# Six of eight blocks of an up-projection with the weights stationary and 256 tokens moving

## The chip, the core and the metric

The kernel runs on one NeuronCore of a Trainium2 chip. Five engines work side by side, each through its own instructions in order: TensorE (PE, which multiplies matrices; its weight loads are listed apart as PEld), VectorE (DVE), ScalarE (ACT), GpSimd (POOL) and SyncE (SP), which here issues nearly all the DMAs. The metric is the device time of one execution in microseconds, less is better.

## The reference

One transformer block on 256 tokens of width 2048: an adaptive normalisation, two attention mixers, an output projection, and a feed-forward part of width 8192. Only the feed-forward part is touched by the change:

```python
h = modulate(rms_norm(x, pre_norm_ffn[l]), shift_f, scale_f)     # 256 x 2048
f = jnp.square(jax.nn.relu(h @ w_up[l])) @ w_down[l]             # w_up 2048 x 8192, w_down 8192 x 2048
x = x + gate_f[:, None, :] * rms_norm(f, post_norm_ffn[l])
```

All of it is in fp32. The kernel splits an operand into a rounded part `hi` (the type fp32r) and a remainder `lo`, and takes three fp32r products, hi·hi, hi·lo and lo·hi, for one product (`products`, L548).

## The kernel before

A matrix multiplication here has a stationary operand of 128 x 128, loaded into PE ahead (LDWEIGHTS), and a moving one of 128 rows and up to 512 columns. The result has the stationary operand's columns as partitions and the moving one's columns along them.

**Up-projection.** The sums over 2048 inputs (16 steps k of 128) run in four groups of four k (`F_GROUPS`, L53; the loop at L1174). In each group eight blocks (`blk`, L1178) of 1024 output features follow one another. For one k of one block `weight_units` (L461) loads 128 x 1024 weights by DMA, splits them into `up_<k>hi` on ACT (L544) and `up_<k>lo` on DVE (L545), and multiplies (`half`, L486): for each of the two halves t of 128 tokens, and for each half ci of 512 features, the tokens (`xmhi`, `modf4hi`, ... and their lo) are stationary and 512 features move. That is 4 PSUM banks per block, one for each (ci, t), and 3 x 4 = 12 matmuls of 512 columns for one k. The banks come in turn from five (`MM_BANKS`, L62), the split weights from five buffers (`WBUFS`, L64), so the weights of a k are split when those of five k earlier are used up. After the fourth k of a block `up_done` (L1153) takes a bank into `facc`: in the first group ACT copies it (L1160), in the others DVE adds it (L1162).

**Transposes.** With the tokens stationary, the sums lie with tokens on the partitions; the down-projection needs features there. So in the last group ACT takes the relu (L1164), and `squares` (L1139) transposes each of the 16 `facc` tiles by eight PE transposes of 128 x 128 (L1146, tile `ft`), which ACT squares on their way back (L1151). Sixteen such groups of eight stand on PE's queue, two inside each block but the first (`later_unit`, L1184) and two at the start of the down-projection (L1294).

**Down-projection.** 64 k of 128 features (`down_units`, L1245, tile `dps`), 24 matmuls of 512 columns each; ahead of every second one `fsplit` (L1197) splits `facc` into `fhi` and `flo`.

**What runs beside.** Inside groups 0 to 2 the scale and shift of the next four k of inputs are summed up on DVE (L323), transposed on PE (L377, `modf4t` in the first group), reduced on DVE (L379, `modf4red`), and put onto the inputs by ACT (L414, L417). A list scheduler puts the program in an order ahead of time, engine by engine; the order on each engine is then fixed.

Of the kernel before, what the change touches and what calls it, by code (L numbers as in the profile page):

```python
# [15 lines left out]
AF = mybir.ActivationFunctionType  # L16
# [3 lines left out]
P = 128  # L20
T = 256
NT = T // P
# [27 lines left out]

M_DIRECT = (3, 7, 11)
F_MODS = (4, 4, 4, 4)
F_GROUPS = ((0, 4), (4, 8), (8, 12), (12, 16))  # L53

F_FIRST = 1
# [3 lines left out]
GATE_K = 54  # L59
# [97 lines left out]
def tile_adaln_block(ctx: ExitStack, tc: tile.TileContext, x, c, w_ada, b_ada, g_pm, g_qm, w_in,  # L157
                     ck_pos, ck_w1, ck_w2, cv_pos, cv_w1, cv_w2, w_o, g_pf, g_qf, w_up, w_down,
                     rope, out):
    nc = tc.nc  # L160
# [101 lines left out]
    stream = Stream()  # L262
# [195 lines left out]
        return [[u] for u in units]  # L458


    def weight_units(name, wap, ks, col0, parts, stat, ps_of, done, spare=(), plain=0):  # L461

        ncol = parts[-1][0] + parts[-1][1]
        units = []
        for i0 in range(0, len(ks), 2):  # L470
            st = {}

            def load(i0=i0, st=st):
                st["raw"] = rawtile(f"{name}_{ks[i0]}")
                k = ks[i0]
                nc.sync.dma_start(
                    st["raw"][:, 0:2 * ncol].rearrange("p (k c) -> p k c", k=2),
                    wap[k * P:(k + 2) * P, col0:col0 + ncol].rearrange("(k p) c -> p k c", p=P))

            for kk in range(2):  # L480
                def prep(st=st, kk=kk, i0=i0):
                    hi, lo = split(st["raw"][:, kk * ncol:(kk + 1) * ncol], f"{name}_{ks[i0] + kk}",
                                   i0 + kk in spare)
                    st[kk] = (hi, lo)

                def half(t, st=st, kk=kk, i=i0 + kk):  # L486
                    k, first, last = ks[i], i == 0, i == len(ks) - 1
                    if k < plain:
                        raw, s32 = st["raw"], stat(k, t)
                    else:  # L490
                        whi, wlo = st[kk]
                        shi, slo = stat(k, t)
                    for ci, (off, wd) in enumerate(parts):
                        b = ps_of(ci, t, first)
                        cs = slice(off, off + wd)
                        if k < plain:
                            nc.tensor.matmul(b[:, 0:wd], s32,
                                             raw[:, kk * ncol + off:kk * ncol + off + wd],
                                             start=first, stop=last)
                        else:  # L500
                            products(b[:, 0:wd], shi, slo, whi[:, cs], wlo[:, cs], first, last)
                        if last:
                            done(ci, t, b)
                    stream.step()

                def main(half=half):
                    for t in range(NT):
                        half(t)

                unsplit = ks[i0] < plain  # L510
                u = Unit(load if kk == 0 else None, None if unsplit else prep, main,
                         w=0 if unsplit or i0 + kk in spare else 1,
                         free=None if kk == 0 else "main" if unsplit else "prep")
                u.half = half
                units.append(u)
        return units
# [28 lines left out]
        nc.vector.tensor_sub(lo[:, 0:n], src, hi[:, 0:n].bitcast(F32))  # L545
        return hi, lo

    def products(o, shi, slo, whi, wlo, first, last):  # L548
        nc.tensor.matmul(o, shi, whi, start=first, stop=False)  # L549
        nc.tensor.matmul(o, shi, wlo, start=False, stop=False)  # L550
        nc.tensor.matmul(o, slo, whi, start=False, stop=last)  # L551

    def banks(name):
        ps = {}
# [418 lines left out]
    def call(f):  # L973
        return [Unit(None, None, f)]
# [85 lines left out]
    def fs(k, t):  # L1060
        hi, lo = fstat[k // 2]
        return hi[:, k % 2, t * P:(t + 1) * P], lo[:, k % 2, t * P:(t + 1) * P]

    x2h = {"mod": {}}

    def keep_mod(k0, n, last):
# [86 lines left out]
    def up_done(blk, g):  # L1153
        def done(ci, t, b):
            n = blk * 2 + ci
            if n not in facc:
                facc[n] = chunk(f"facc{n}")
            dst = facc[n][:, t, :]
            if g == 0:
                nc.scalar.copy(dst, b)  # L1160
            else:
                nc.vector.tensor_add(dst, b, dst)  # L1162
            if g == len(F_GROUPS) - 1:
                nc.scalar.activation(dst, dst, AF.Relu)  # L1164
                if t == NT - 1:
                    later.append(n)
        return done

# [5 lines left out]
    for g, span in enumerate(F_GROUPS):  # L1174
# [3 lines left out]
        for blk in range(NB):  # L1178
            name = f"up{g}_{blk}"
            spare = ((1,), (1, 3))[blk] if g == 0 and blk < 2 else ()  # L1180
            us = weight_units(name, w_up, ks, blk * 1024, C2, fs, banks(name), up_done(blk, g),
                              spare)
            if lastg and blk:
                us = us[:2] + call(later_unit) + us[2:4] + call(later_unit) + us[4:]  # L1184
            base += us
        extra = [u for i, m in enumerate(ffn_mods) for u in m
# [58 lines left out]
    def down_units(k):  # L1245
# [31 lines left out]
        def half(t, order=(0, 1, 2, 3)):  # L1277
            hi, lo = fst[k // 2]
            ts_ = slice(t * P, (t + 1) * P)
            for n in order:  # L1280
# [10 lines left out]

    dn = [down_units(k) for k in range(KF)]
    token_major(dn[-4:], finish, 4)
    stream.add(2 * call(later_unit)  # L1294
               + spread(dn[:GATE_K], gf, 4, GATE_K - 2) + dn[GATE_K:GATE_K + 4]
               + [Unit(free="main")] + dn[GATE_K + 4:])
    stream.run()

# [24 lines left out]
```

## Time and profile before

| | |
|---|---|
| three runs, us | 1187.60, 1188.22, 1189.65; median 1188.22 |
| the profiled execution | 1188.98 us, of which the span of the core 1187.2 |
| PE busy in the span | 1154.3 us, 5411 matmuls |
| DVE, ACT busy | 901.4 and 592.8 us |
| DMA | 312 MB, 263 GB/s |
| up-projection, first to last matmul on the trace | about 457 to 825 us |
| down-projection | about 826 to 1180 us |

Busy time on PE counts pipelined matmuls whose ends are modelled, so that what a matmul costs is read from the distance between the starts of two that follow one another.

### The profile page before, as it was taken

How to read it: one execution, taken by the hardware profiler on the slowest of the kernel's cores; microseconds unless marked ns; L12 is line 12 of the kernel's file. 1: busy time of each engine (PE TensorE's matmuls, PEld its weight loads, DVE VectorE, ACT ScalarE, POOL GpSimd, SP SyncE). 2: the span in 40 equal slices, each digit the busy share in tenths (PEclk: the TensorE clock that was granted, in tenths of full speed). 3: DMA queues.
4: the chain of work that ended last, by engine and by line, in shares of the span. 5: the costliest groups of instructions: out<-in, count | busy, mean ns of one | idle time of the engine just before them, and what ended most of it. 6: DMA issues, size and time to landing. Idle time of an engine off the chain costs nothing.

```text
span 1187.2 us, 14413 instructions
## 1 busy us (share of the span) xinstructions
PE 1154.3 (97%) x5411; PEld 935.7 (79%) x5411; DVE 901.4 (76%) x1111; ACT 592.8 (50%) x908; POOL 13.5 (1%) x23
## 2 busy tenths in 40 slices
PE   5999999999999998999999999999999999999997
PEld 4468888877777786888888888888888888888885
DVE  5679999889999988777888986666576666665573
ACT  4353444438746658565343344767444434444441
POOL 1000000000000001000000000000000000000000
PEclk9999999999999999999999999999999999999999
DMA  9999998775867985988878976545677777775541
GB/s 333 370 394 326 334 362 295 238 281 176 316 213 258 327 337 200 367 285 305 290 249 300 315 248 204 172 152 208 238 244 270 255 258 264 259 268 187 203 142 71
DMA packets 92601, 312.03 MB, mean 263 GB/s; under 512 B 6306, under 2 KB 14962, under 8 KB 79602
## 3 DMA queue, kind: packets, MB, share of 16 engines
q1 hardware_dynamic: 92324, 311.04, 74.7%
q8 instruction: 42, 0.69, 0.2%
q14 instruction: 27, 0.22, 0.1%
q10 hardware_dynamic: 208, 0.07, 0.0%
HBM read 308.99 MB, written 2.10 MB: 262 GB/s over the span
## 4 chain that ended last, share of the span: by engine, by line
PE 88%; DVE 7%; ACT 1%; issue 1%; DMA 1%; POOL 0%; SPq 0%; DVEq 0%; POOLq 0%; ACTq 0%
PE dps L550 10%; PE dps L551 10%; PE dps L549 10%; PE up L551 9%; PE up L550 9%; PE up L549 9%; PE wo L550 2%; PE wo L549 1%; PE wo L551 1%; PE ft L1146 1%; PE in_qm L551 1%; PE in_qm L549 1%; PE in_qm L550 1%; PE in_km L549 1%; PE in_km L550 1%
## 5 line engine op out<-in xcount | busy, mean ns | idle before, releaser
L323 DVE SCALAR_TENSOR_TENSOR modm<-modm,csil,modm 128x1024 f32<-128x1024 f32 (+1 forms) x72 | 78.3, 1087 | 9.4 <-DMA modm<-in_w_ada_dram 8.0
L323 DVE SCALAR_TENSOR_TENSOR modf<-modf,csil,modf 128x1024 f32<-128x1024 f32 x60 | 76.8, 1280 | 5.6 <-DMA modf<-in_w_ada_dram 5.2
L1162 DVE TENSOR_TENSOR facc<-up,facc 128x512 f32<-128x512 f32 x96 | 61.5, 685 | 19.2 <-PE up L551 19.2
L323 DVE SCALAR_TENSOR_TENSOR gatef<-gatef,csil,gatef 128x1024 f32<-128x1024 f32 x32 | 40.6, 1280 | 1.7 <-DMA gatef<-in_w_ada_dram 1.7
L323 DVE SCALAR_TENSOR_TENSOR gatem<-gatem,csil,gatem 128x1024 f32<-128x1024 f32 x32 | 40.3, 1275 | 0.0
L1202 DVE TENSOR_TENSOR flo<-facc,fhi 128x512 fp32r<-128x512 f32 x32 | 21.8, 686 | 2.0 <-ACT fhi L1201 2.0
L1201 ACT CAST fhi<-facc 128x512 fp32r<-128x512 f32 x32 | 19.7, 624 | 5.3 <-PE up L550 1.9
L1164 ACT ACTIVATE facc<-facc 128x512 f32<-128x512 f32 x32 | 18.4, 623 | 2.8 <-DVE facc L1162 2.8
L1160 ACT COPY facc<-up 128x512 f32<-128x512 f32 x32 | 18.0, 586 | 1.7 <-PE up L551 1.0
L545 DVE TENSOR_TENSOR up_13lo<-up,up_13hi 128x1024 fp32r<-128x1024 f32 x8 | 9.8, 1226 | 11.5 <-ACT up_13hi L544 11.5
L545 DVE TENSOR_TENSOR up_14lo<-up,up_14hi 128x1024 fp32r<-128x1024 f32 x8 | 9.8, 1226 | 11.1 <-ACT up_14hi L544 11.1
L1151 ACT ACTIVATE facc<-ft 128x512 f32<-128x512 f32 x32 | 17.1, 586 | 0.4 <-PE ft L1146 0.2
L1146 PE MATMUL ft<-ident,facc 128*128 128x128 f32 x128 | 16.8, 273 | 0.0
L1146 PEld LDWEIGHTS ft<-ident,facc 128*128 128x128 f32 x128 | 14.7, 140 | 2.6 <-ACT facc L1151 0.4
L544 ACT CAST up_7hi<-up 128x1024 fp32r<-128x1024 f32 x8 | 8.4, 1056 | 14.2 <-PE up L551 14.2
L544 ACT CAST up_11hi<-up 128x1024 fp32r<-128x1024 f32 x8 | 8.4, 1056 | 14.2 <-PE up L551 14.2
L544 ACT CAST up_10hi<-up 128x1024 fp32r<-128x1024 f32 x8 | 8.4, 1056 | 13.3 <-PE up L551 13.3
L544 ACT CAST up_6hi<-up 128x1024 fp32r<-128x1024 f32 x8 | 8.4, 1056 | 13.3 <-PE up L551 13.3
L544 ACT CAST up_14hi<-up 128x1024 fp32r<-128x1024 f32 x8 | 8.4, 1049 | 12.6 <-PE up L551 12.6
L544 ACT CAST up_9hi<-up 128x1024 fp32r<-128x1024 f32 x8 | 8.4, 1056 | 12.1 <-DVE up_8lo L545 6.7
L544 ACT CAST up_8hi<-up 128x1024 fp32r<-128x1024 f32 x8 | 8.4, 1054 | 11.7 <-PE up L551 11.7
L544 ACT CAST up_5hi<-up 128x1024 fp32r<-128x1024 f32 x8 | 8.4, 1056 | 11.2 <-PE up L551 7.8
(2266 smaller groups left out, 3966.4 us busy)
## 6 DMA issues: line engine op xcount, KB each, us to landing
up<-in_w_up_dram SPq DMA_DIRECT2D x64, 1024.0 KB, 5.2
dn<-in_w_down_dram SPq DMA_DIRECT2D x64, 1024.0 KB, 5.0
modf<-in_w_ada_dram SPq DMA_DIRECT2D x64, 512.0 KB, 6.2
modm<-in_w_ada_dram SPq DMA_DIRECT2D x48, 512.0 KB, 7.1
gatem<-in_w_ada_dram SPq DMA_DIRECT2D x16, 1024.0 KB, 5.5
wo<-in_w_o_dram SPq DMA_DIRECT2D x16, 1024.0 KB, 6.3
gatef<-in_w_ada_dram SPq DMA_DIRECT2D x16, 1024.0 KB, 4.9
modm<-in_w_ada_dram SPq DMA_DIRECT2D x32, 256.0 KB, 6.0
```

Of the source, the lines that this page charges most:

```text
L323: nc.vector.scalar_tensor_tensor(part, w[:, j:j + step], csil[:, k:k + 1], part, ALU.mult, ALU.add)
L544: nc.scalar.copy(hi[:, 0:n], src)
L545: nc.vector.tensor_sub(lo[:, 0:n], src, hi[:, 0:n].bitcast(F32))
L549: nc.tensor.matmul(o, shi, whi, start=first, stop=False)
L550: nc.tensor.matmul(o, shi, wlo, start=False, stop=False)
L551: nc.tensor.matmul(o, slo, whi, start=False, stop=last)
L1146: nc.tensor.transpose(b[:, (2 * i + t) * P:(2 * i + t + 1) * P], f[:, t, (2 * j + i) * P:(2 * j + i + 1) * P], ident)
L1160: nc.scalar.copy(dst, b)
L1162: nc.vector.tensor_add(dst, b, dst)
L1164: nc.scalar.activation(dst, dst, AF.Relu)
L1201: nc.scalar.copy(hi, f)
L1202: nc.vector.tensor_sub(lo, f, hi.bitcast(F32))
```

## The change

In blocks 2 to 7 of every group the operands change places: 128 features of the weights are stationary and all 256 tokens move. A matmul has 256 columns in place of 512, and there are 24 for one k in place of 12. A bank (ci, t) now holds 2 x 128 features on the partitions and 256 tokens along each, which is the layout that the down-projection wants; so ACT takes the relu and then the square in place (L1189 of the changed kernel), and `squares` is left for the four `facc` tiles of blocks 0 and 1 alone. The two calls at the start of the down-projection go. Loads, splits, banks, and copies or adds out of the banks stay as many and as large as they were.

```diff
+UP_TOKENS = 2
@@ weight_units
+                    if across:
+                        whi, wlo = st[kk]
+                        xhi, xlo = stat(k)
+                        for ci, (off, wd) in enumerate(parts):
+                            b = ps_of(ci, t, first)
+                            for j in range(2):
+                                o = off + (2 * t + j) * P
+                                cs = slice(o, o + P)
+                                products(b[:, j * T:(j + 1) * T], whi[:, cs], wlo[:, cs], xhi, xlo,
+                                         first and j == 0, last, skip_group_check=True)
+                            if last:
+                                done(ci, t, b)
+                        stream.step()
+                        return
@@
+    def fs_all(k):
+        hi, lo = fstat[k // 2]
+        return hi[:, k % 2, :], lo[:, k % 2, :]
@@ up_done
             if g == len(F_GROUPS) - 1:
                 nc.scalar.activation(dst, dst, AF.Relu)
-                if t == NT - 1:
+                if blk >= UP_TOKENS:
+                    nc.scalar.activation(dst, dst, AF.Square)
+                elif t == NT - 1:
                     later.append(n)
@@
-            us = weight_units(name, w_up, ks, blk * 1024, C2, fs, banks(name), up_done(blk, g),
-                              spare)
-            if lastg and blk:
+            across = blk >= UP_TOKENS
+            us = weight_units(name, w_up, ks, blk * 1024, C2, fs_all if across else fs, banks(name),
+                              up_done(blk, g), spare, across=across)
+            if lastg and 0 < blk <= UP_TOKENS:
                 us = us[:2] + call(later_unit) + us[2:4] + call(later_unit) + us[4:]
@@
-    stream.add(2 * call(later_unit)
-               + spread(dn[:GATE_K], gf, 4, GATE_K - 2) + dn[GATE_K:GATE_K + 4]
+    stream.add(spread(dn[:GATE_K], gf, 4, GATE_K - 2) + dn[GATE_K:GATE_K + 4]
```

PE at the end of the up-projection, before: the last bank of block 7 (`up_7_1_1`, k 15), then transposes, which go on between the first matmuls of the down-projection (`dps`).

```order
L549 MATMUL up_7_1_1_6880<-up_7_15hi,modf12hi_6046 128x512
L550 MATMUL up_7_1_1_6880<-up_7_15lo,modf12hi_6046 128x512
L551 MATMUL up_7_1_1_6880<-up_7_15hi,modf12lo_6047 128x512
L1146 MATMUL ft_6964<-ident,facc_4726 128x128 x4
L1146 MATMUL ft_6969<-ident,facc_4726 128x128 x4
L1146 MATMUL ft_6976<-ident,facc_4799 128x128
L549 MATMUL dps_7001<-dn00hi,fhi_6920 128x512
L550 MATMUL dps_7001<-dn00lo,fhi_6920 128x512
L551 MATMUL dps_7001<-dn00hi,flo_6921 128x512
```

The same place in the changed kernel (L568 to L570 are its lines of `products`):

```order
L568 MATMUL up_7_1_1_7917<-modf12hi_6838,up_7_15hi 128x256
L569 MATMUL up_7_1_1_7917<-modf12lo_6839,up_7_15hi 128x256
L570 MATMUL up_7_1_1_7917<-modf12hi_6838,up_7_15lo 128x256
L568 MATMUL up_7_1_1_7917<-modf12hi_6838,up_7_15hi 128x256
L569 MATMUL up_7_1_1_7917<-modf12lo_6839,up_7_15hi 128x256
L570 MATMUL up_7_1_1_7917<-modf12hi_6838,up_7_15lo 128x256
L568 MATMUL dps_8032<-dn00hi,fhi_7924 128x512
L569 MATMUL dps_8032<-dn00lo,fhi_7924 128x512
L570 MATMUL dps_8032<-dn00hi,flo_7925 128x512
```

Three matmuls of 512 columns became six of 256, and the first product of the down-projection follows the last of the up-projection directly.

The scheduler also moves other work a little. ACT in the first group, before, at the end of block 4: the four copies out of block 4's banks (`facc<-up_4_...`) stand ahead of the work on the next inputs (`xnf`, `modf4hi`).

```order
L544 CAST up_5_3hi<-up_5_2_4418 128x1024
L1160 COPY facc_4526<-up_4_0_0_4459 128x512
L1160 COPY facc_4531<-up_4_1_0_4463 128x512
L1160 COPY facc_4526<-up_4_0_1_4467 128x512
L1160 COPY facc_4531<-up_4_1_1_4471 128x512
L414 ACTIVATE xnf_3920<-xnf_3920,modf4red 128x256 x2
L414 ACTIVATE xnf_3921<-xnf_3921,modf4red 128x256
```

ACT at the same place in the changed kernel:

```order
L563 CAST up_5_3hi<-up_5_2_4490 128x1024
L416 ACTIVATE xnf_3920<-xnf_3920,modf4red 128x256 x2
L416 ACTIVATE xnf_3921<-xnf_3921,modf4red 128x256
L419 CAST modf4hi_4901<-xnf_3920 128x512
L416 ACTIVATE xnf_3921<-xnf_3921,modf4red 128x256
L1183 COPY facc_4661<-up_4_0_0_4555 128x512
L419 CAST modf4hi_4907<-xnf_3921 128x512
L1183 COPY facc_4669<-up_4_1_0_4562 128x512
```

The copies now stand behind that work. On PE the eight transposes `modf4t` moved from the fourth k of block 4 into its third.

## Rows read from the trace of the kernel before

**Rows 1.** The page: busy time by engine; the granted clock in 40 slices.

```profile
PE 1154.3 (97%) x5411; PEld 935.7 (79%) x5411; DVE 901.4 (76%) x1111; ACT 592.8 (50%) x908; POOL 13.5 (1%) x23
...
PEclk9999999999999999999999999999999999999999
```

**Rows 2.** The page: the chain that ended last, by engine.

```profile
PE 88%; DVE 7%; ACT 1%; issue 1%; DMA 1%; POOL 0%; SPq 0%; DVEq 0%; POOLq 0%; ACTq 0%
```

**Rows 3.** Stages: window, length; busy PE, PEld, DVE, ACT, POOL; clock; DMA; GB/s.

```profile
550.00:630.00 80.00, 80.00 (x358) 66.28 (x357) 68.72 (x77) 34.59 (x37) 0.00 (x0) 1.00 0.81 285
630.00:737.00 107.00, 107.00 (x477) 88.61 (x476) 88.14 (x97) 44.71 (x46) 1.82 (x1) 1.00 0.76 263
737.00:825.00 88.00, 88.00 (x442) 73.97 (x442) 57.44 (x67) 61.06 (x89) 0.00 (x0) 1.00 0.52 178
...
832.00:1180.00 348.00, 346.45 (x1528) 286.40 (x1526) 211.21 (x204) 149.20 (x168) 0.55 (x1) 1.00 0.64 224
```

**Rows 4.** Waits of PE, whole span: us, times, longest.

```profile
PE up L549 <- ACT xmhi L417: 1.1, 1, 1.1
PE up L550 <- DVE up_2lo L545: 1.0, 1, 1.0
```

**Rows 5.** Waits of all engines, 550 to 640 us.

```profile
ACT up_7hi L544 <- PE up L551: 12.5, 7, 2.6
```

**Rows 6.** Line 1146: durations in ns, first and last start.

```profile
L1146 PE MATMUL ft<-ident,facc x128: 270/272/329, 742.7 to 830.4; 128*128 128x128 f32 x128
```

**Rows 7.** Timeline of PE around one group of transposes: start, length, instruction.

```profile
742.48 0.39 PE L551 MATMUL up<-up_13hi,modf12lo 128*128 128x512 f32 x1
742.71 1.03 PE L1146 MATMUL ft<-ident,facc 128*128 128x128 f32 x8
743.50 0.48 PE L549 MATMUL up<-up_14hi,modf12hi 128*128 128x512 f32 x1
...
744.28 0.39 PE L549 MATMUL up<-up_14hi,modf12hi 128*128 128x512 f32 x1
```

**Rows 8.** Timeline of PE from the up- to the down-projection.

```profile
825.04 1.14 PE L1146 MATMUL ft<-ident,facc 128*128 128x128 f32 x9
...
834.05 0.39 PE L551 MATMUL dps<-dn10hi,flo 128*128 128x512 f32 x1
```

**Rows 9.** Timeline of PE, 512 columns: the first and the 51st in a row.

```profile
700.55 0.39 PE L549 MATMUL up<-up_10hi,modf8hi 128*128 128x512 f32 x1
...
711.88 0.39 PE L551 MATMUL up<-up_10hi,modf8lo 128*128 128x512 f32 x1
```

**Rows 10.** Timeline of PE, 268 columns: the first and the 25th in a row.

```profile
117.07 0.28 PE L549 MATMUL in_kw<-in_kw_2hi,modm2hi 128*128 128x268 f32 x1
...
119.97 0.28 PE L549 MATMUL in_kw<-in_kw_4hi,modm2hi 128*128 128x268 f32 x1
```

**Rows 11.** Timeline of PE's weight loads just after the transposes of rows 7.

```profile
743.48 0.19 PEld L549 LDWEIGHTS up<-up_14hi,modf12hi 128*128 128x128 f32 x1
743.59 0.19 PEld L550 LDWEIGHTS up<-up_14lo,modf12hi 128*128 128x128 f32 x1
```

**Rows 12.** Timeline of ACT at the end of block 4, first group.

```profile
514.17 1.05 ACT L544 CAST up_3hi<-up 128x1024 fp32r<-128x1024 f32 x1 [1.67 <-PE up L551]
515.13 0.57 ACT L1160 COPY facc<-up 128x512 f32<-128x512 f32 x1
516.67 1.96 ACT L1160 COPY facc<-up 128x512 f32<-128x512 f32 x3 [0.97 <-PE up L551]
518.53 1.59 ACT L414 ACTIVATE xnf<-xnf,modf4red 128x256 f32<-128x256 f32 x3
520.02 0.61 ACT L417 CAST modf4hi<-xnf 128x512 fp32r<-128x512 f32 x1
520.53 0.61 ACT L414 ACTIVATE xnf<-xnf,modf4red 128x256 f32<-128x256 f32 x1
```

**Rows 13.** The page, costliest groups: busy us, mean ns, idle before.

```profile
L1164 ACT ACTIVATE facc<-facc 128x512 f32<-128x512 f32 x32 | 18.4, 623 | 2.8 <-DVE facc L1162 2.8
...
L1151 ACT ACTIVATE facc<-ft 128x512 f32<-128x512 f32 x32 | 17.1, 586 | 0.4 <-PE ft L1146 0.2
```

More of the change, by code (lines that the diff above doesn't have):

```diff
@@ L458, in gate_units, with weight_units @@
         return [[u] for u in units]
-    def weight_units(name, wap, ks, col0, parts, stat, ps_of, done, spare=(), plain=0):
+    def weight_units(name, wap, ks, col0, parts, stat, ps_of, done, spare=(), plain=0,
+                     across=False):
         ncol = parts[-1][0] + parts[-1][1]
@@ L546, in split, with products @@
         return hi, lo
[L548 to L551, printed above, removed]
+    def products(o, shi, slo, whi, wlo, first, last, **kw):
+        nc.tensor.matmul(o, shi, whi, start=first, stop=False, **kw)
+        nc.tensor.matmul(o, shi, wlo, start=False, stop=False, **kw)
+        nc.tensor.matmul(o, slo, whi, start=False, stop=last, **kw)
     def banks(name):
```

## The prediction

> **What bounds the kernel now.** I read the busy times first, then the chain that ended last, then the stages, and in the stages the waits. PE is busy 97% of the span at the full clock of 2.4 GHz [rows 1], and it carries 88% of the chain [rows 2]. Stage by stage the up-projection is PE from end to end: 80.0 of 80 us, 107.0 of 107 and 88.0 of 88; in the down-projection 346.5 of 348, while in these four stages DVE is busy for at most 86% of the time, ACT for 69% and the DMA engines for 81% [rows 3]. The waits say the same from the other side: over the whole span PE waits for the up-projection's operands twice, 1 us each, at its start [rows 4], and it is ACT that waits for PE to give weight buffers back, 12.5 us on one tile's casts alone within 90 us [rows 5]. So in this part the time is the sum of what stands on PE's queue, and an instruction taken off it or put on it counts nearly in full.
>
> **What the change takes away.** Twelve of the sixteen groups of eight transposes (128 transposes in all) [rows 6]. What a group costs is not its 1.03 us of busy time but the delay of what follows: from the matmul at 742.48 to the one at 744.28 there are 1.80 us; four distances of 226.6 ns (below) would be 0.906; the rest, 0.89 us, is the price of eight transposes with what they do to the matmul after them [rows 7]. Blocks 1 and 2 keep four groups. Of the other twelve, ten stand among matmuls in the last group of k and cost 10 x 0.89 = 8.9 us. At the seam to the down-projection there are 24 transposes, three groups, one of them counted in the ten: from 825.04 to 834.05 only 26 matmuls were started, and 9.01 - 26 x 0.2266 = 3.12 us were lost [rows 8], so two groups with their stalls are 3.12 - 0.89 = 2.2 us. Together **11.1 us** go. ACT loses 24 squares of 586 ns and gets 24 of about 623, the length of the relu on the same tile [rows 13]: 0.9 us more on an engine that is busy 61 of 88 us there [rows 3], so nothing. The squares stand behind the relu on ACT's queue and hold casts back, but as long as the squares before did; the banks are freed by DVE's add, ahead of both.
>
> **What it adds on PE.** In 6 blocks x 16 k, 12 matmuls of 512 columns become 24 of 256: 1152 pairs in place of 1152 matmuls. The columns are as many; the price is what a pair takes beyond the one. Fifty distances at 512 columns are 711.88 - 700.55 = 11.33 us, 226.6 ns each [rows 9]. No row has 256 fp32r columns; the nearest are 268, with a fresh stationary operand for each, just as the changed kernel has: 24 distances in 2.90 us, 120.8 ns [rows 10]. That bounds it from above, as fewer columns don't take longer. From below, half of 226.6 is 113.3 ns. Between them: a straight line through 268 and 512 columns rises 0.434 ns a column and gives 115.6 at 256. If all of a matmul's time is its columns, a pair costs nothing more; by the line it costs 2 x 115.6 - 226.6 = 4.6 ns, or 5.3 us over 1152; by the 268 columns themselves 15.0 ns, or 17.3 us. I take the middle of the first two, 114.5 ns: +2.4 ns a pair, **+2.8 us**.
>
> **Is the weight load hidden?** The records of loads are 0.19 us, longer than 114.5 ns, but they overlap. After transposes, with nothing left to hide behind, one load starts at 743.48 and the next at 743.59, when the first is through: 110 ns [rows 11]. That is below 113.3, so at 256 columns a load still fits behind the matmul before it, by 3 to 5 ns. This is the thin place of the change: at 512 columns there were over 100 ns to spare. A gain below zero on this term would need a matmul under 113.3 ns, and the load's 110 is its floor.
>
> **What it moves.** Loads by SP are in the same order, so no DMA is moved past another. The scheduler moved the modulation of the next inputs. At the end of block 4 of the first group, four copies out of PSUM now stand on ACT behind four activations and a cast, and these behind the cast of `up_5_3hi`, which needs the buffer of block 4's third k. Counted from the start of block 4: a k is 24 x 114.5 ns = 2.75 us; the third ends, with eight transposes in it, at 3 x 2.75 + 0.89 = 9.1; the cast takes 1.05, the activations and casts ahead of the first copy 1.59 + 0.5 + 0.5 us, the copy 0.57 [rows 12], so the first bank is empty at about 13.3 with some 0.5 us of passing on. PE is through with the block at 11.9, fills the fifth bank for 0.69 us, and asks for the first at 12.6. It waits 0.7, and about 0.3 more for the second, which has another cast ahead of it. I take **+1.0 us**, once, between 0 (the scheduler's order turned out to fit) and 2 (each bank late). The same count in the next two groups, where DVE adds, finds the banks empty 0.5 us or more ahead of PE, so nothing. At the seam, DVE frees the four banks of block 7 between 0.5 and 2.4 us after its end, ahead of their use at 1.4, 2.0, 2.7 and 3.4: nothing either; what hid this before, the transposes, is gone, and 1 us of lateness there would cost 1 us.
>
> **Sum.** -11.1 + 2.8 + 1.0 = -7.3 us. The profiled execution took 1188.98 us (span 1187.2), 0.76 above the median of the runs; its own time would become 1181.7, and the median 1188.22 becomes **1180.9 us**. The ends of the same case are -11.1 (pair for nothing, no stall) and -11.1 + 5.3 + 2.0 = -3.8: 1177.1 to 1184.4.
>
> **Rivals.** First, **the load sets the pace**. The 268 columns could take 120.8 ns because two operands are fetched at once or a load is swapped in late, not for their columns; then 256 take as long, the pair costs 15.0 ns, and the sum is -11.1 + 17.3 + 1.0 = +7.2 us: 1195.4, slower. It decides from 117.7 ns a matmul, where 1152 pairs have eaten 10.1 us. For it: the load's record of 0.19 us, and that the margin is 3 to 5 ns. Against it: 110 ns when bare, and 120.8 is close to what the columns give (268/512 of 226.6 is 118.6). Chance 0.12.
>
> Second, **the surplus of the long matmuls goes**. 512 columns at 2.4 GHz are 213.3 ns, and 226.6 are measured; were the 13 ns something that short matmuls don't have, only the load's 110 ns would remain: 1152 x (220 - 226.6) = -7.6, in all -17.7 us, 1170.5. Against it stand the 268 columns, 9 ns above their 111.7 [rows 10]. Chance 0.03. The Trainium skill, "TensorE: Matmul & The Clock Gate", section "Back-to-back issue gap", states such a rule: columns over 2.4 GHz plus 2.5 ns, an estimate of 109.2 ns at 256, by which the sum would be -19.5 us; the same rule gives 215.8 at 512, where this trace has 226.6.
>
> Third, **loads stand in line with matmuls**. Then each of 1152 added loads costs its 110 ns, +127 us, about 1305. It would have shown already: 268 columns with a load each would take 222 ns, and take 120.8 [rows 10]. Chance 0.01. The same page says, in "Part 3: Packing small matmuls — row/col tiling", that a load overlaps running matmuls only on other row groups of the array; every matmul here uses all rows, and this trace doesn't agree. (Its Part 2 also allows a load into a background buffer, which the rows do fit.)
>
> Fourth, **the gain isn't passed on**: the last group of k shrinks from 88 to about 78 us and the next limit, weights by DMA, shows. It would have to move 178 x 88/78 = 201 GB/s where 285 and 263 were reached before [rows 3]; time about as now, 1188. Chance 0.04.
>
> **How the numbers follow.** The forecast's case has 0.80. The range takes in its ends with 1 us for what a run differs, and on the upper side the way from 115.6 towards the 117.7 ns at which the sign turns: 1176 to 1187. Left out are the first rival, the second, the third and the fourth: 0.20. 0.2% is 2.4 us, about what a measurement of this kernel can tell from no change. The forecast's case ends at -3.8 and lies beyond that, so faster has 0.80 + 0.03, less 0.02 for matmuls between 115.6 and 117.7 ns: 0.81; within 0.2% 0.04 + 0.02 = 0.06; slower 0.13.
>
> **What would show it.** In the trace after: L1146's successor with 32 transposes, not 128; matmuls of 128x256 in `up` starting 113.3 to 115.6 ns apart (at 120 the first rival holds); one short wait of PE on a copy of `facc` near 515 us; the first `dps` directly behind the last `up`; waits of ACT on PE as now. Groups 0 to 2 of k together would be about 3 us longer than before, the last group about 8 shorter, the seam 2 shorter, and the down-projection as long as it was. The prediction is wrong if the spacing leaves that band, or if PE shows waits in `up` that add up to more than 2 us.

## The result and the profile after

The changed kernel is slower: 1198.39 us median against 1188.38 us on the same chip, 10.0 us more. Over all the runs the ratio is 1.0076 (95% interval 1.0060 to 1.0093), which is 9.0 us. The prediction was 7 us less. The profiled execution took 1198.31 us (span 1196.5), 9.3 more than that of before.

The page of the changed kernel, busy time by engine, answers to [rows 1]. PE has 1056 instructions more (1152 added matmuls less 96 transposes) and 4 us more of busy time:

```profile
PE 1158.4 (97%) x6467; PEld 985.7 (82%) x6467; DVE 901.5 (75%) x1111; ACT 593.0 (50%) x908; POOL 13.5 (1%) x23
```

The stages of the changed kernel, columns as in [rows 3]. The up-projection is still PE from end to end at full clock, but for 2.5 us in the first window:

```profile
550.00:630.00 80.00, 77.55 (x558) 72.91 (x557) 63.17 (x70) 33.42 (x37) 0.00 (x0) 1.00 0.75 262
630.00:737.00 107.00, 107.00 (x809) 103.14 (x808) 87.18 (x96) 41.77 (x43) 1.82 (x1) 1.00 0.76 266
737.00:825.00 88.00, 88.00 (x653) 84.12 (x652) 56.76 (x65) 60.47 (x85) 0.00 (x0) 1.00 0.53 179
```

Fixed windows don't say which stage grew, since the work shifts through them. For that I took the first matmul of each group of k and of the down-projection from PE's timeline (start, length, instruction), first of the kernel before:

```profile
457.27 0.39 PE L549 MATMUL up<-up_0hi,xmhi 128*128 128x512 f32 x1
550.49 0.39 PE L549 MATMUL up<-up_4hi,modf4hi 128*128 128x512 f32 x1
638.42 0.39 PE L549 MATMUL up<-up_8hi,modf8hi 128*128 128x512 f32 x1
726.39 0.39 PE L549 MATMUL up<-up_12hi,modf12hi 128*128 128x512 f32 x1
825.94 0.48 PE L549 MATMUL dps<-dn00hi,fhi 128*128 128x512 f32 x1
```

and then of the changed kernel:

```profile
459.12 0.39 PE L568 MATMUL up<-up_0hi,xmhi 128*128 128x512 f32 x1
556.08 0.40 PE L568 MATMUL up<-up_4hi,modf4hi 128*128 128x512 f32 x1
651.04 0.40 PE L568 MATMUL up<-up_8hi,modf8hi 128*128 128x512 f32 x1
742.86 0.40 PE L568 MATMUL up<-up_12hi,modf12hi 128*128 128x512 f32 x1
837.25 0.40 PE L568 MATMUL dps<-dn00hi,fhi 128*128 128x512 f32 x1
```

The differences of these starts, in us (the last stage runs to the end of the span):

| stage | before | after | difference |
|---|---|---|---|
| up to the up-projection | 457.27 | 459.12 | +1.85 |
| group 0 of k | 93.22 | 96.96 | +3.74 |
| group 1 | 87.93 | 94.96 | +7.03 |
| group 2 | 87.97 | 91.82 | +3.85 |
| group 3, with the transposes | 99.55 | 94.39 | -5.16 |
| down-projection to the end | 361.26 | 359.25 | -2.01 |

Three readings explain the table. The first is the distance of the 256-column matmuls. In PE's timeline of the changed kernel these two are 81 distances apart:

```profile
702.19 0.29 PE L568 MATMUL up<-modf8hi,up_9hi 128*128 128x256 f32 x1
...
711.90 0.28 PE L568 MATMUL up<-modf8hi,up_9hi 128*128 128x256 f32 x1
```

9.71 us over 81 is 119.9 ns, and to the nanosecond nearly every distance is 120. A pair costs 2 x 120 - 226.6 = 13.4 ns more than the matmul that it replaces, 288 pairs in a group 3.86 us, which is groups 0 and 2; all 1152 cost **15.4 us**.

The second is the transposes. Group 3 is 5.16 shorter although its pairs took 3.86 more: 9.0 us went there, and 2.0 behind it, as predicted (8.9 and 2.2).

The third is group 1, 3.2 us beyond its pairs. PE's waits in the up-projection (us, times, longest) have a line that [rows 4] don't have, and its timeline shows where:

```profile
PE up L568 <- DVE facc L1185: 2.4, 2, 1.7
```

```profile
567.44 0.39 PE L570 MATMUL up<-up_4hi,modf4lo 128*128 128x512 f32 x1
569.51 0.50 PE L568 MATMUL up<-up_4hi,modf4hi 128*128 128x512 f32 x1 [1.68 <-DVE facc L1185]
...
570.08 0.40 PE L570 MATMUL up<-up_4hi,modf4lo 128*128 128x512 f32 x1
571.25 0.50 PE L568 MATMUL up<-up_4hi,modf4hi 128*128 128x512 f32 x1 [0.77 <-DVE facc L1185]
```

The two waits are 2.4 of the 3.2 us. PE wants a PSUM bank that DVE's add into `facc` (line 1185) has to empty. The add itself takes 0.69 us; DVE's timeline shows what stands ahead of it:

```profile
565.24 1.28 DVE L325 SCALAR_TENSOR_TENSOR modf<-modf,csil,modf 128x1024 f32<-128x1024 f32 x1 [3.90 <-DMA modf<-in_w_ada_dram]
566.44 1.22 DVE L564 TENSOR_TENSOR up_6lo<-up,up_6hi 128x1024 fp32r<-128x1024 f32 x1
567.57 1.28 DVE L325 SCALAR_TENSOR_TENSOR modf<-modf,csil,modf 128x1024 f32<-128x1024 f32 x1
568.77 0.69 DVE L1185 TENSOR_TENSOR facc<-up,facc 128x512 f32<-128x512 f32 x1
```

DVE sat 3.90 us in front of a product for the modulation; everything behind it on DVE's queue, the add among it, was late. SP issued that product's DMA at 558.63 in the changed kernel, 2.55 us after the first matmul of group 1, and at 551.55 in the kernel before, 1.06 us after it. Why SP came later isn't shown. Over the whole run DVE waits 17.4 us for these DMAs, and 5.2 in the kernel before. DVE's row of before for the product shows a wait of 1.16 us, and PE waits for nothing there:

```profile
556.88 1.28 DVE L323 SCALAR_TENSOR_TENSOR modf<-modf,csil,modf 128x1024 f32<-128x1024 f32 x1 [1.16 <-DMA modf<-in_w_ada_dram]
```

Of the +1.85 before the up-projection, some 1.6 is a stretch of 3.4 us at half clock (1.2 GHz) in the output projection, far from the change. Just ahead of it PE had waited 1.96 us for split weights; at the same place it waited 1.64 us in the kernel before, and kept its clock. The window of the changed kernel, columns as above:

```profile
416.90:420.20 3.30, 3.30 (x13) 2.92 (x12) 2.20 (x4) 1.04 (x1) 0.00 (x0) 0.50 0.99 389
```

The profiled execution of before has 1.00 there and a mean clock of 0.998 over the span; its other executions on another chip have means from 0.990 up, as the changed kernel's (0.991 to 0.995). I don't count this stretch as the change's.

So: 15.4 + 3.2 - 11.0 + 1.85 = 9.4, against the 9.3 of the two executions. The 3.2 us are read from one execution of each kernel.

### The profile page after: what moved, and what is told of

It is laid out like the page before. It is cut to its first block, busy times and chain, and to the rows that moved or that the text cites. A ratio compares the mean times of both kernels' runs of the same rounds, so it can differ in the third digit from the quotient of the medians.

```text
span 1196.5 us, 16542 instructions
## 1 busy us (share of the span) xinstructions
PE 1158.4 (97%) x6467; PEld 985.7 (82%) x6467; DVE 901.5 (75%) x1111; ACT 593.0 (50%) x908; POOL 13.5 (1%) x23
## 4 chain that ended last, share of the span: by engine, by line
PE 86%; DVE 8%; DMA 2%; issue 2%; ACT 1%; POOL 0%; SPq 0%; ACTq 0%; DVEq 0%; POOLq 0%
PE dps L570 10%; PE dps L569 10%; PE dps L568 10%; PE up L568 10%; PE up L569 9%; PE up L570 9%; PE wo L569 2%; PE wo L570 2%; PE wo L568 1%; PE in_qm L570 1%; PE in_qm L568 1%; PE in_qm L569 1%; DVE modm L325 1%; PE in_km L568 1%; PE in_km L569 1%
## 5 line engine op out<-in xcount | busy, mean ns | idle before, releaser
L325 DVE SCALAR_TENSOR_TENSOR modf<-modf,csil,modf 128x1024 f32<-128x1024 f32 x60 | 76.9, 1282 | 17.7 <-DMA modf<-in_w_ada_dram 17.4
L1187 ACT ACTIVATE facc<-facc 128x512 f32<-128x512 f32 x32 | 18.9, 624 | 3.3 <-DVE facc L1185 3.3
L563 ACT CAST up_6hi<-up 128x1024 fp32r<-128x1024 f32 x8 | 8.4, 1049 | 15.3 <-PE up L569 10.2
L563 ACT CAST up_9hi<-up 128x1024 fp32r<-128x1024 f32 x8 | 8.4, 1052 | 13.7 <-PE up L569 10.2
L563 ACT CAST up_15hi<-up 128x1024 fp32r<-128x1024 f32 x8 | 8.4, 1049 | 12.0 <-PE up L569 9.8
L1189 ACT ACTIVATE facc<-facc 128x512 f32<-128x512 f32 x24 | 14.3, 623 | 0.2
L564 DVE TENSOR_TENSOR up_2lo<-up,up_2hi 128x1024 fp32r<-128x1024 f32 x8 | 9.8, 1224 | 5.3 <-ACT up_2hi L563 5.3
L568 PE MATMUL up<-modf12hi,up_12hi 128*128 128x256 f32 x48 | 13.7, 286 | 0.0
```

The lines of the kernel that those rows point to most:

```text
L325: nc.vector.scalar_tensor_tensor(part, w[:, j:j + step], csil[:, k:k + 1], part, ALU.mult, ALU.add)
L563: nc.scalar.copy(hi[:, 0:n], src)
L568: nc.tensor.matmul(o, shi, whi, start=first, stop=False, **kw)
L1189: nc.scalar.activation(dst, dst, AF.Square)
```

## The experiments

Each ran beside the kernel before on the same chip. The diffs show the lines that matter; lines that only hand a new argument on are left out.

### Halving alone

```diff
+CUTS = {blk: (256, 256) for blk in range(2, 8)}
-                            products(b[:, 0:wd], shi, slo, whi[:, cs], wlo[:, cs], first, last)
+                            at = 0
+                            for n in cuts or (wd,):
+                                products(b[:, at:at + n], shi, slo, whi[:, off + at:off + at + n],
+                                         wlo[:, off + at:off + at + n], first and at == 0, last, ...)
+                                at += n
```

> The kernel before, tokens stationary as ever, with each matmul of 512 columns in blocks 2 to 7 split into two of 256; transposes stay. Same result, 1152 more matmuls, no change of operands. Theory L (a fresh 128 x 128 fp32r stationary operand lets the next matmul start 120 ns later at the soonest) and theory C (256 to 268 columns simply take 120 ns): spacing 120 ns, 1152 x 13.4 ns = +15.4 us, about 1204. Theory O (what costs is the exchange of the operands, weights stationary and tokens moving): spacing at or under 115.6 ns, at most +5.3 us, 1188 to 1194.

Measured: 1208.95 us, ratio 1.0160 (1.0127 to 1.0193). The tokens stay stationary, the transposes stay, and 66 distances at 256 columns take 7.90 us, 119.7 ns each:

```profile
702.02 0.29 PE L556 MATMUL up<-up_9hi,modf8hi 128*128 128x256 f32 x1
...
709.92 0.28 PE L556 MATMUL up<-up_8hi,modf8hi 128*128 128x256 f32 x1
```

So the price is that of cutting a matmul in two. Exchanging the operands is neither dearer nor cheaper: theory O falls, and L and C, which both said 120 ns, are told apart by the widths below. Groups 0, 2 and 3 are 3.7, 4.2 and 3.5 us longer than in before (3.86 by the pairs), and group 1 is 6.2 longer, with 1.0 us of PE waiting for the same add and 0.6 for products of the modulation: the stall comes without the exchange of the operands too.

### The transposes alone

The kernel before, without the transposes of blocks 2 to 7; they are left out, and the squares are taken in place.

```diff
-                if t == NT - 1:
+                if blk >= 2:
+                    nc.scalar.activation(dst, dst, AF.Square)
+                elif t == NT - 1:
                     later.append(n)
@@
-            if lastg and blk:
+            if lastg and 0 < blk <= 2:
@@
-    stream.add(2 * call(later_unit)
-               + spread(dn[:GATE_K], gf, 4, GATE_K - 2) + dn[GATE_K:GATE_K + 4]
+    stream.add(spread(dn[:GATE_K], gf, 4, GATE_K - 2) + dn[GATE_K:GATE_K + 4]
```

> The kernel before without the transposes of blocks 2 to 7: ACT squares in place, so the down-projection reads tiles that weren't transposed (left out: 96 transposes). All else as before. This is what the change takes away, alone. The prediction's step: -11.1 us, about 1177. Rival: without that cover the seam waits for copies out of the banks or for weights, and less than 8 us go, above 1180.

Measured: 1180.91 us, ratio 0.9918 (0.9897 to 0.9939). Group 3 is 8.95 us shorter than in before, the stage behind it 2.2. The first matmul of the down-projection follows the last of the up-projection at once:

```profile
819.87 0.39 PE L551 MATMUL up<-up_15hi,modf12lo 128*128 128x512 f32 x1
820.09 0.39 PE L549 MATMUL dps<-dn00hi,fhi 128*128 128x512 f32 x1
```

The 11.1 us of the prediction are 11.15 by the stages. By the ratio 9.8 us went, with an interval from 7.3 to 12.3; the medians lie 10.1 apart. Group 1, which the edit doesn't touch, is 0.9 us longer in this execution: that much of a stage can be chance.

### What a matmul costs by its width

The kernel before with its 512 columns cut unevenly: in the first kernel 320+192, 384+128, 288+224, 272+240, 448+64 and 256+256 in blocks 2 to 7, in the second 268+244, 260+252, 264+248, 304+208 and 336+176 with block 7 uncut. The edit is that of the halves with other numbers:

```diff
+CUTS = {2: (320, 192), 3: (384, 128), 4: (288, 224), 5: (272, 240), 6: (448, 64),
+        7: (256, 256)}
```

> The kernel before with the matmuls of 512 columns cut unevenly, each block its own way: block 2 in 320 + 192, block 3 in 384 + 128, block 4 in 288 + 224, block 5 in 272 + 240, block 6 in 448 + 64, block 7 in 256 + 256. Same result; the spacing after each width is read from the trace. Theory L: 64, 128, 192, 224, 240, 256 columns all 120 ns; from about 277 columns on the columns rule, 0.434 ns each: 288 about 129, 320 about 143, 384 about 171, 448 about 199. Theory C: the short ones fall with their columns, 240 about 112, 192 about 90, 128 about 60, or stop at the bare load's 110 ns.

```diff
+CUTS = {2: (268, 244), 3: (260, 252), 4: (264, 248), 5: (304, 208), 6: (336, 176),
+        7: (512,)}
```

> The kernel before with the 512 columns of blocks 2 to 6 cut unevenly: 268+244, 260+252, 264+248, 304+208, 336+176; block 7 uncut. Same sums. It asks what a matmul of about 268 columns costs in this stage. Law L (columns / 2.4 + 13.3 ns at full clock): 260: 121.6, 264: 123.3, 268: 125.0, 304: 140.0, 336: 153.3 ns from one start to the next of its own kind. Theory S (steps: what the in_kw row showed, 268 columns in 120.8 ns, holds everywhere, and from 256 to 268 the spacing is flat): 120 to 121 ns for 260, 264 and 268 alike, and a straight line from 268 to 512 of 0.434 ns a column above. By S the prediction's row was good and its line below 268 wrong; by L the row does not carry over from in_kw. About 1210 to 1225 us by either, since the number of matmuls is that of e1_halves.

They took 1272.88 and 1259.99 us (one execution each), where the second expectation said 1210 to 1225. Besides the short matmuls, which cost more than their share of the columns, PE waits in the up-projection 28 and 41 us for adds and modulation products of DVE, and behind such waits the granted clock is at half for a time. The question was the distances. PE's timeline of the second kernel, one cut of 268 and 244 columns (the last two matmuls of each):

```profile
600.43 0.28 PE L558 MATMUL up<-up_4lo,modf4hi 128*128 128x268 f32 x1
600.55 0.28 PE L559 MATMUL up<-up_4hi,modf4lo 128*128 128x268 f32 x1
...
600.78 0.28 PE L558 MATMUL up<-up_4lo,modf4hi 128*128 128x244 f32 x1
600.89 0.28 PE L559 MATMUL up<-up_4hi,modf4lo 128*128 128x244 f32 x1
```

The median distance from the middle one of three equal matmuls to the third, at full clock, over both kernels (50 distances or more each; left out are 176, 208, 224, 244 and 248 columns, at 111.5 to 114 ns, and 272, 288 and 320, at 127, 135 and 146; columns / 2.4 is what the columns take at 2.4 GHz):

| columns | 64 | 128 | 192 | 240 | 252 | 256 | 260 | 264 | 268 | 304 | 336 | 384 | 448 | 512 |
|---|---|---|---|---|---|---|---|---|---|---|---|---|---|---|
| ns | 110 | 111 | 113 | 114 | 114 | 120 | 122 | 121 | 123 | 140 | 152 | 174.5 | 202 | 227 |
| columns / 2.4 | 26.7 | 53.3 | 80 | 100 | 105 | 106.7 | 108.3 | 110 | 111.7 | 126.7 | 140 | 160 | 186.7 | 213.3 |
| beyond | | | | | | 13.3 | 13.7 | 11 | 11.3 | 13.3 | 12 | 14.5 | 15.3 | 13.7 |

From 256 columns up a matmul takes its columns and 11 to 15 ns, whatever its width. Below that, nothing goes under 110 to 114 ns, about the 110 of a bare load in [rows 11], and so theory C of the first kernel holds with its floor, and theory L's 120 ns for all of them falls. The fixed part doesn't reach below 256: 248 and 252 columns, at 113 and 114 ns, take 9 to 10 ns beyond their columns. Neither theory of the second kernel holds to the nanosecond (260, 264 and 268 columns stand at 122, 121 and 123 ns, up to 2.3 under L's law and up to 2.2 over S's flat 120.8), and the law of a fixed part comes within 2.3 ns everywhere between 256 and 448.

### 128 columns

The changed kernel with 128 tokens moving in three of four k; the products of the other tokens are left out.

```diff
+MOVED = 128
-                                products(b[:, j * T:(j + 1) * T], whi[:, cs], wlo[:, cs], xhi, xlo,
+                                m = T if first else MOVED
+                                products(b[:, j * T:j * T + m], whi[:, cs], wlo[:, cs],
+                                         xhi[:, 0:m], xlo[:, 0:m],
```

> The changed kernel with 128 tokens moving in place of 256 in three of the four k of each group, blocks 2 to 7 (left out: half of those columns' products). 1728 matmuls are half as long. Theory L: spacing stays at 120 ns and the time at the changed kernel's, about 1198. Theory C: spacing about 60 ns, or the bare load's 110 ns: 1728 x 10 to 60 ns = 17 to 104 us less, 1094 to 1181.

Measured: 1257.98 us, ratio 1.0568, slower than the kernel with all of its columns. The distance has the answer: at full clock 71 of them take 7.88 us, 111 ns each, which is theory C with the bare load's 110 ns. Group 3, where PE never waits and the clock stays at full, takes 90.8 us for the changed kernel's 94.4, and 432 matmuls of 9 ns less are 3.9.

The time went elsewhere, and neither theory had it. In groups 0 to 2 PE waits 36.7 us for DVE, which in its turn sits 52.3 us in front of modulation products whose DMA hasn't landed. Two of these waits in PE's list:

```profile
PE up L571 <- DVE facc L1188: 13.8, 5, 4.0
PE modf4t L380 <- DVE modf L326: 10.3, 1, 10.3
```

And the granted clock is at half (1.2 GHz) for 92 us, in eight stretches. Each of them begins while PE waits, or 0.1 us after a wait. The longest begins at 662.0, in a wait that ends at 662.64. PE's timeline shows that wait and both speeds, and the window the clock:

```profile
662.64 0.58 PE L571 MATMUL up<-modf4hi,up_4hi 128*128 128x256 f32 x1 [2.29 <-DVE facc L1188]
...
666.76 0.41 PE L572 MATMUL up<-modf4lo,up_5hi 128*128 128x128 f32 x1
...
675.94 0.41 PE L573 MATMUL up<-modf4hi,up_6lo 128*128 128x128 f32 x1
...
686.59 0.22 PE L571 MATMUL up<-modf4hi,up_5hi 128*128 128x128 f32 x1
...
694.47 0.28 PE L573 MATMUL up<-modf4hi,up_7lo 128*128 128x128 f32 x1
```

```profile
662.00:682.00 20.00, 19.36 (x91) 19.36 (x91) 11.47 (x13) 3.20 (x4) 0.00 (x0) 0.50 0.67 232
```

So 111 ns, about the bare load of [rows 11], is the floor for this kernel's short matmuls, and 120 at 256 columns is not that floor. At half clock it is 213 ns. That the load makes the floor is read from the two equal numbers; no kernel had short matmuls with narrower loads.

### What the fixed part belongs to

Three kernels asked whether the 13 ns come with the type of the operands or with the load that runs under the matmul before. The first reads three quarters of the changed kernel's operands as bf16 (the lower halves are left out):

```diff
+                                ops = whi[:, cs], wlo[:, cs], xhi, xlo
+                                if not first:
+                                    ops = [v.bitcast(BF16)[:, 1::2] for v in ops]
```

> The changed kernel with the operands of blocks 2 to 7, save for the first k of each sum, read as bfloat16 (the upper halves of the same words, at a stride of two); the lower halves are left out. 864 of the 1,152 matmuls of 256 columns in each... of the group's 288 three quarters are changed. It asks whose the fixed 13.3 ns are. Theory F (they belong to fp32r: a bf16 matmul of 272 columns stands 116 ns from the next, 2.5 ns over 272 / 2.4): 109 to 110 ns, so 864 x 10.5 ns = 9 us less than the changed kernel, about 1189, if the clock stays full. Theory W (they belong to the width or to the load that stands in the gap): 120 ns, 1198. A clock that falls, as in e4_128_columns, would spoil the total; the spacing at full clock decides.

The second loads fewer columns (the products of the others are left out):

```diff
+STAT = {2: 96, 3: 96, 4: 64, 5: 64, 6: 32, 7: 32}
+                                m = P if first else STAT[col0 // 1024]
+                                cs = slice(o, o + m)
+                                products(b[0:m, j * T:(j + 1) * T], whi[:, cs], wlo[:, cs], xhi, xlo,
```

> The changed kernel with fewer stationary columns in three quarters of the matmuls of blocks 2 to 7: 96 in blocks 2 and 3, 64 in 4 and 5, 32 in 6 and 7; the products of the other weight columns are left out. 256 columns move as before. It asks whether the fixed 13.3 ns come from the load that runs under the matmul before. Theory V (the load takes its share out of the stream, by its columns): 116.7 ns at 96, 113.3 at 64, 110 at 32; about 1193 us. Theory F (they belong to an fp32r matmul, whatever is loaded): 120 ns at each, 1198 us.

The third puts both questions at 512 columns, on the kernel before:

```diff
+                            ops, m = (shi, slo, whi[:, cs], wlo[:, cs]), P
+                            if name.startswith("up") and not first and 2048 <= col0 < 5120:
+                                ops = [v.bitcast(BF16)[:, 1::2] for v in ops]
+                            elif name.startswith("up") and not (first or last) and col0 >= 5120:
+                                m = 64
+                                ops = [v[:, 0:m] for v in ops[:2]] + list(ops[2:])
+                            products(b[0:m, 0:wd], *ops, first, last)
```

> The kernel before with matmuls of 512 columns throughout. In blocks 2 to 4 the operands of all but the first k of a sum are read as bfloat16 (upper halves at a stride of two, lower halves left out). In blocks 5 to 7 the two middle k have 64 stationary columns in place of 128 (the products of the other 64 tokens are left out). At 512 columns the load lies well inside the matmul before, so the floor of 110 to 113 ns can't hide anything, as it may have at 256. Theory F (the fixed 13.3 ns belong to an fp32r matmul): 215.8 ns in bf16 (512 / 2.4 + 2.5, from the bf16 matmuls of 272 columns at 116 ns), 226.6 ns with 64 stationary columns. Theory V (they come from the load under the matmul before): about 220 ns with 64 stationary columns, and 220 to 227 in bf16. The total is not the question: 864 / 2 x 11 ns = 5 us less for blocks 2 to 4 by F, up to 2 us less for blocks 5 to 7 by V.

The first expectation's 864 are pairs: 1728 matmuls are changed, and the saving that F names would be 18 us. They took 1189.28 us (ratio 0.9992, 0.9980 to 1.0005), 1192.50 (1.0022, 1.0011 to 1.0032) and 1190.20 (one execution). First and last rows of a stretch in PE's timeline: the bf16 kernel over 51 distances, the narrow loads over 71 (96 columns), 30 (64) and 70 (32):

```profile
697.78 0.28 PE L573 MATMUL up<-modf8hi,up_9lo 128*128 128x256 bf16 x1
...
703.56 0.28 PE L573 MATMUL up<-modf8hi,up_11lo 128*128 128x256 bf16 x1
```

```profile
591.79 0.28 PE L570 MATMUL up<-modf4hi,up_5hi 128*96 128x256 f32 x1
600.03 0.27 PE L572 MATMUL up<-modf4hi,up_7lo 128*96 128x256 f32 x1
...
607.51 0.28 PE L572 MATMUL up<-modf4hi,up_5lo 128*64 128x256 f32 x1
610.93 0.28 PE L572 MATMUL up<-modf4hi,up_6lo 128*64 128x256 f32 x1
...
627.81 0.28 PE L571 MATMUL up<-modf4lo,up_5hi 128*32 128x256 f32 x1
636.05 0.28 PE L572 MATMUL up<-modf4hi,up_7lo 128*32 128x256 f32 x1
```

That is 113.3 ns for bf16 (1728 x 6.6 ns = 11 us; the medians differ by 9), and 116.1, 114.0 and 117.7 ns for the narrow loads (means; at 96 columns the single distances run from 112 to 121). At 512 columns, 23 distances each:

```profile
719.32 0.40 PE L555 MATMUL up<-up_9hi,modf8hi 128*64 128x512 f32 x1
724.61 0.39 PE L557 MATMUL up<-up_10hi,modf8lo 128*64 128x512 f32 x1
...
770.02 0.39 PE L555 MATMUL up<-up_14hi,modf12hi 128*128 128x512 bf16 x1
775.20 0.39 PE L557 MATMUL up<-up_15hi,modf12lo 128*128 128x512 bf16 x1
```

230 ns with 64 stationary columns (V said 220) and 225.2 in bf16 (F said 215.8). Both theories fall: the fixed part is there in bf16, with 12 ns at 512 columns, and it doesn't shrink in step with the columns that are loaded. At 256 columns either edit brings the distance down to within 8 ns of the load's floor. One rival is left untested: these bf16 operands were read at a stride of two. In the kernel before, bf16 matmuls of 272 columns among the attention scores, read without a stride, stand 116 ns ahead of the next matmul, 2.7 beyond their columns (the first at 268.60 us, the next matmul at 268.71). So in bf16 the 12 ns may be the stride's. What the 13 ns are made of stays open; that the fp32r matmuls of this stream have 11 to 15 ns beyond their columns, from 256 to 512 of them, is measured.

### The stall of group 1

```diff
-        start = 8 if g == 0 else 2
+        start = 8 if g == 0 else 6
```

> The changed kernel with the last DMA units of w_ada in groups 1 and 2 of the up-projection put four steps later in their group (start 6 in place of 2), nothing else. It asks whether the stall of group 1 is one of order on VectorE. Theory D (the facc add stands behind the two scalar_tensor_tensor that wait for w_ada's DMA; PE pays 2.4 + 2 + 1.7 us for it, some 3 us net): the adds pass, the group 1 stage goes from 94.96 us to 92 or less, and the kernel to about 1195 (ratio to before 1.0050 to 1.0060 in place of 1.0076). Rival R (the DMA is late for reasons of its own, bandwidth or its ring, and another wait follows): group 1 stays at 94 to 95 and the time at 1198. Both say the change stays slower than before by the 15.4 us of the fixed part less the 11.1 us of the transposes.

Measured: 1196.93 us, ratio 1.0064 (1.0046 to 1.0082) where the changed kernel has 1.0076; the intervals overlap. By the stages group 1 takes 92.97 us, 2.0 less, but group 2 takes 93.10, 1.3 more. PE's waits in the up-projection and the rows with the adds of DVE at the old place:

```profile
PE up L568 <- DVE facc L1185: 1.6, 3, 0.8
```

```profile
561.49 2.62 DVE L325 SCALAR_TENSOR_TENSOR modf<-modf,csil,modf 128x1024 f32<-128x1024 f32 x2 [1.95 <-DMA modf<-in_w_ada_dram]
...
565.16 0.69 DVE L1185 TENSOR_TENSOR facc<-up,facc 128x512 f32<-128x512 f32 x1
```

Both were half right. The add comes sooner when it doesn't stand behind the product that waits for its DMA, so the stall is one of order on DVE (D); but moving the product puts it ahead of another add, one group on (DVE waits 1.62 us for the DMA of the product at 669.06, the adds begin at 670.26, and PE has waited 0.45 us when its next matmul starts at 671.00), and by the stages 2.5 of the 3.2 us are paid all the same (R). These are single executions, and a stage can move by 0.9 us without an edit; that the time of the kernel fell is not shown.

### One block instead of six

```diff
-UP_TOKENS = 2
+UP_TOKENS = 7
```

> The changed kernel with UP_TOKENS 7 in place of 2: only the last block has its weights stationary, the seven others are as in the kernel before. Ledger A (each turned block costs 192 pairs x 13.4 ns = 2.57 us and saves two groups of transposes, 2 x 0.89 us; the 2.2 us between the up-projection and the down-projection go as soon as the last block is turned, however many others are): 2.57 - 1.78 - 2.2 = -1.4 us, ratio to before 0.9988, the last group's stage longer by 0.64 - 1.78 = -1.1 us, the stage after it shorter by 2.0 to 2.2 us. Rival B (the 2.2 us there need all six blocks, since the squares of the last blocks then stand inside the up-projection one after the other): +0.8 us, ratio 1.0007, and the stage after the up-projection as before, 361 us.

Measured: 1191.67 us, ratio 1.0010 (0.9999 to 1.0022): no difference from the kernel before is shown, and A's gain (0.9988) is outside of the interval. Expectation A counted the last two groups of transposes twice: they are the 2.2 us of the seam, and no others go when only block 7 is turned. The right sum of the same prices is 2.57 - 2.2 = +0.4 us; the stages have +0.63, +0.66, +1.2, +0.5 in the four groups and -2.1 behind them, +0.9 together. B's mechanism falls, since the stage behind the up-projection is 359.2 us and not 361. At the seam stands one group of transposes where before there were three [rows 8]:

```profile
829.98 1.03 PE L1169 MATMUL ft<-ident,facc 128*128 128x128 f32 x8
830.77 0.48 PE L568 MATMUL dps<-dn00hi,fhi 128*128 128x512 f32 x1
```

By these prices no number of turned blocks beats the kernel before: each costs 192 pairs, 2.57 us, and spares two groups, 1.79 us; the first one gives 2.2 for its 2.57. Only one and six were run.

## Why the prediction was wrong

**What bounds the kernel** held, save for the stall of group 1. In the up-projection an instruction on PE counts in full; both the loss of 15.4 us and the gain of 11 reached the end of the kernel.

**The transposes** held: -11.1 us predicted, -11.0 in the changed kernel, -11.15 alone. To price them by the distances around them and not by their busy time was right.

**The pairs are the step that failed.** The term was +2.8 us and measured +15.4. Two choices made it small. The lower end, half of 226.6, takes for granted that everything in a matmul's 226.6 ns shrinks with its columns. But 512 columns at the granted 2.4 GHz are 213.3 ns, as the second rival says, so 13.3 ns were something else. I saw these 13.3 ns, and used them only in the rival in which short matmuls don't have them. If every matmul has them, 256 columns take 106.7 + 13.3 = 120.0 ns, and that is what they take. The second choice was the straight line through 268 and 512 columns. Its slope, 0.434 ns a column, is above the 0.417 of one column per cycle at 2.4 GHz (the widths above rise by 0.418 from 256 to 512), and should have shown that the two rows don't lie on one line: so steep a line leaves only some 4.5 ns for the fixed part. The 268-column row belongs to another stage with 120.8 ns; in the up-projection the same width takes 123. Why it is shorter there stays open. The outer bound, 120.8, was the nearest row by far, and I gave it 0.12.

**The weight load** held as a bound: 110 ns when bare, and 110 to 114 under every width from 64 to 252. It fits behind 256 columns, as the prediction said; it isn't what makes the 120 ns there, since 252 columns pass in 114.

**The waits.** The +1.0 us in group 0 didn't come: group 0 is longer by its pairs alone, and PE has no wait on a copy of `facc` there. In groups 1 and 2 the prediction found the banks empty in time, and in group 1 that was wrong by 3.2 us. It counted the lengths of DVE's instructions, but not that one ahead of the add waits for a DMA. The term was predicted +1.0 and measured +3.2, at another place. The fourth rival's "last group of k" of 88 us is the window of [rows 3]; the group itself took 99.6 and went to 94.4.

**The rivals.** The first had nearly the right price (120.8 ns for 120) and the right sign, but not its mechanism: the floor lies at 110 to 114, and above it the distance goes by the columns, 121 to 227 ns from 260 to 512 of them, with the fixed part on top. How much of the fixed part at 256 columns hangs on the load isn't settled: with 64 stationary columns it was 114.0 ns. The turning point, 117.7 ns, was good. The second fails: the surplus of the long matmuls is there at 256 columns too. The rule of the Trainium skill named with it ("TensorE: Matmul & The Clock Gate", section "Back-to-back issue gap") gives 2.5 ns beyond the columns; here it is 11 to 15. The section gives it for a matmul by itself, and says that in a stream of loads and matmuls both set the distance, so it bore on this term less than the prediction lets it appear. Loads in line, and a limit behind PE, aren't seen: 120 ns is far from 222, and group 3 is as short as its instructions say.

**The sum by the measured prices**, 15.4 - 11.0 + 3.2 = +7.6 us, gives 1195.8 from the median before, slower and outside of the range. The medians lie 10.0 apart, and the ratio says 9.0: 1.4 to 2.4 us have no row here; in the profiled pair 1.85 us came ahead of the up-projection, most of them from the clock.

## What to carry to other kernels

When a matmul is to be cut, take the distance at the old width, subtract the columns at the granted clock, and give the rest to every piece until a row shows otherwise; a line through rows of two stages that rises faster than one column per cycle is not to be trusted. Fewer transposes are worth their distance on PE, which is little beside a cost that every matmul of the stage pays. When PE waits for a bank to be emptied, look not at the emptying instruction but at what stands ahead of it in its queue, and whether that waits for a DMA.

## What the hardware showed beyond that

- In this stream an fp32r matmul of 256 to 512 columns costs 11 to 15 ns beyond its columns, and 12 ns in bf16 at a stride of two and 512 columns. Below 256 columns a matmul takes 110 to 114 ns, about a bare load, be it 252 columns or 64.
- The clock of these streams fell when PE had to wait. In the kernel with 128 columns and the two with uneven cuts PE waited for DVE, and all 17 half-clock stretches in their up-projections began in such a wait or within 0.5 us of its end. The longest was 23.9 us at 0.50, and a matmul of 128 columns took 213 ns there in place of 111. In the changed kernel, whose longest wait in the up-projection was 1.7 us, the clock stayed at 1.00 over the whole of it.
- With 32 stationary columns a matmul of 256 took 117.7 ns, more than with 64 (114.0) or 96 (116.1), though the records of the loads shrink with their columns (192 ns at 128, 108 at 32). No theory here explains it.
